# Strassen's seven block products for part of a feed-forward's first multiplication

## The chip, the core and the metric

The kernel runs on one core of a Trainium2 chip. A core has TensorE (matrix products from SBUF into the eight PSUM banks), VectorE, ScalarE and GpSimd (elementwise work), and SyncE, whose queue issues nearly all DMAs of this kernel. The metric is the device time of one execution in microseconds; lower is better. The median of three runs before the change is 756.35 us (755.69 to 757.19).

## The reference, cut to what matters

A layer of a trunk for 512 tokens of width 1024: a token mixer with four groups of heads (mLSTM, short convolution, block attention, HGRN2), a cross-attention to 256 memory rows, and a gated feed-forward, each between two rmsnorms with a residual. The change is in the feed-forward:

```python
def conv_glu_ffn(xn, w_up, conv_w, conv_b, w_down):   # 1024 -> 2 x 2816 -> 1024
    gu = xn @ w_up
    gate, up = jnp.split(gu, 2, axis=-1)
    gate = causal_dwconv(gate, conv_w) + conv_b.astype(gate.dtype)   # 3 taps along the tokens
    return (jax.nn.silu(gate) * up) @ w_down
...
    h = conv_glu_ffn(rmsnorm(x, norm_ffn_pre[l]), ...)
    x = x + rmsnorm(h, norm_ffn_post[l])
```

All data are fp32.

## The kernel before

Products are made in the type fp32r. To keep fp32's accuracy each operand is split into a high part (a rounded copy, written by ScalarE) and a low part (the rest, subtracted by VectorE; `split`, line 483, and `stage`, line 488, for weights), and a product is three matmuls: high x high, high x low, low x high (`three`, line 480).

The normalised tokens lie transposed in `xTh` and `xTl` (partition = channel within one of 8 blocks, columns = 4 token tiles of 128). `norm_T` (line 572) makes them: rms, scaling, a transposition on TensorE into PSUM, and a split. The feed-forward takes the 2816 channels in 22 tiles of 128 (`NF`, loop at line 1138). For a tile f it stages two weight blocks (gate j = 0, up j = 1; 512 KB each), runs 8 x 3 matmuls of 512 columns for each into a PSUM bank, applies the three taps (`act`, two `stt`), Silu and the multiply by `up`, and splits the result into `hT`, which stays in SBUF. Tile 0 alone works on token halves of 256 columns, so that it can begin before the last two token tiles are normalised. The second products (`down`, line 1180) come after all first products (`after=[up_]`): 22 tiles x 4 token tiles x 2 column halves x 3 matmuls of 512 columns, accumulated in all eight banks. The last three tiles are done token tile by token tile, each followed by `residual` (line 1040), which adds to `X[t]` and stores the output.

The order on every engine is worked out by a planner in the program (`Plan`, `schedule`, line 209). Each operation has a cost (`mcost`, line 451, for a matmul; `act`, `dcost` for the others), the planner simulates the engines and the buffers, and always takes the operation that can start earliest; between equals the one with the longest remaining path plus its `boost`. Buffers come from fixed numbers of slots by size: 33 of 4 KB and 10 of 2 KB per partition, and 8 PSUM banks (`SLOTS`, line 38). A unit of operations starts only when the slots that it needs at once are free. A `quota` limits live buffers of a kind (weights 8 tiles ahead for f < 2, then 4; three raw blocks `st`), and a `fifo` keeps the order of loads and of splits. What the planner puts on an engine is executed in that order.

Of the kernel before, what the change touches and what calls it, by code (L numbers as in the profile page):

```python
# [26 lines left out]
P = 128  # L27
# [92 lines left out]
class Plan:  # L120
# [221 lines left out]
def kernel(  # L342
    ctx, tc, x, mem, w_in, b_in, mlstm_norm, rel_bias, hgrn_lb_logits, hgrn_norm,
    w_mix_out, norm_mix_pre, norm_mix_post, mem_norm, w_cq, w_ck, w_cv, w_co,
    norm_cross_pre, norm_cross_post, w_ffn_in, w_ffn_out,
    norm_ffn_pre, norm_ffn_post, c_f, c_m, cols_in, scratch, out,
):
    nc = tc.nc
    pl = Plan()
# [107 lines left out]
    def mms(o, terms, first=True, last=True, spare=0, n=None, quota=(), after=(), boost=0.0, fifo=None, cold=1):  # L457

        def go():
            for j, (l, r) in enumerate(terms):  # L460
                i = nc.tensor.matmul(o.ap(), l.ap(), r.ap(), start=first and j == 0,  # L461
                                     stop=last and j == len(terms) - 1)
# [106 lines left out]
    xTl = sb([P, NT, KT, P], FR, "xTl")  # L569

    @unit
    def norm_T(src, g, dst):
        xs = [sb([P, 512], FT, "xs") for _ in range(2)]
        r = rms([src[:, h * 512:(h + 1) * 512] for h in range(2)], xs)
        for h in range(2):
            hs = slice(h * 512, (h + 1) * 512)
            stt(xs[h].all, src[:, hs], r[:, 0:1], g[:, hs], OP.mult, OP.mult)
        for h in range(2):
            p = ps([P, 4, P])
            for k in range(4):  # L580
# [513 lines left out]
    for t in range(NT):  # L1094
        pl.boost = -5000.0 * t
        qh, ql = qT[t // 2]
        tq = slice((t % 2) * P, (t % 2) * P + P)
        oh_, ol_ = sb([P, 4, P], FR, "oh"), sb([P, 4, P], FR, "ol")
        for hp in range(2):
            with pl.unit():  # L1100
                sp, mx, pr = ps([P, 2, 256]), sb([P, 4], FT, "cmx"), sb([P, 2, 256], FT, "cpr")
                for hh in range(2):
                    h = hp * 2 + hh
                    mms(sp[:, hh, :], three(qh[:, h, tq], ql[:, h, tq], ckh[:, h, :], ckl[:, h, :]), n=256)
                rmax(mx[:, 0:2], sp.all)
# [12 lines left out]
                for hh in range(2):  # L1118
                    h = hp * 2 + hh
                    mms(oT[:, hh, :], [(cv[:, m, h * P:(h + 1) * P], pt[:, hh, m, :]) for m in range(2)])  # L1120
                split(oh_[:, 2 * hp:2 * hp + 2, :], ol_[:, 2 * hp:2 * hp + 2, :], oT.all)
        with pl.unit():
            pp = []
            for c in range(2):
                p, cs = ps([P, 512]), slice(c * 512, c * 512 + 512)
                for k in range(4):
                    wh, wl = wo[k]
                    mms(p.all, three(oh_[:, k, :], ol_[:, k, :], wh[:, 0, cs], wl[:, 0, cs]), k == 0, k == 3,
                        spare=BIG)
                pp.append(p)  # L1130
            xo2 = residual(pp, g_cpost, t)
        norm_T(X[t], g_fpre, into(t))


    pl.boost = 0.0
    g_fpost = gain(norm_ffn_post, [xo2])
    hT = []
    for f in range(NF):
        ww = [stage(wsrc(w_ffn_in, 0, KT, j * DFF + f * P, P), [P, KT, P], 8 if f < 2 else 4) for j in range(2)]
        with pl.unit():  # L1140
            pp = []
            for j in range(2):
                p = ps([P, S])
                wh, wl = ww[j]
                halves = [slice(0, 2), slice(2, 4)] if f < 1 else [slice(0, 4)]
                for hv_ in halves:
                    for k in range(KT):
                        o = p[:, hv_.start * P:hv_.stop * P]
                        up_ = mms(o, three(wh[:, k, :], wl[:, k, :], xTh[:, hv_, k, :], xTl[:, hv_, k, :]),
                                  k == 0, k == KT - 1)  # L1150
                pp.append(p)
            pg, pu = pp
            if f < 4:
                hh, hl = [sb([P, S], FR, "hT") for _ in range(2)]
                vh, vl = hh.all, hl.all
            else:
                hb = sb([P, 2, S], FR, "hT")
                vh, vl = hb[:, 0, :], hb[:, 1, :]
            hT.append((vh, vl))
            w = [cols[:, 22 + 22 * j + f:23 + 22 * j + f] for j in range(3)]  # L1160
            fc = sb([P, S], FT, "fc")
            act(fc.all, pg.all, AF.Copy, scale=w[2])
            stt(fc[:, 1:], pg[:, :S - 1], w[1], fc[:, 1:], OP.mult, OP.add)
            stt(fc[:, 2:], pg[:, :S - 2], w[0], fc[:, 2:], OP.mult, OP.add)
            act(fc.all, fc.all, AF.Silu, bias=cols[:, 88 + f:89 + f])
            tt(fc.all, fc.all, pu.all, OP.mult)
            split(vh, vl, fc.all)

    NL = 3
    wd = []  # L1170
    for f in range(NF):
        src = flat(w_ffn_out, f * P * D, [[D, P], [1, D]])
        if f >= NF - 4:
            i = f - (NF - 4)
            wd.append(stage(src, [P, D], 4, into=(xTh[:, i].re("p k i -> p (k i)"), xTl[:, i].re("p k i -> p (k i)"))))
        else:
            hb, lb2 = stage(src, [P, D], 4)
            wd.append((hb.all, lb2.all))

    def down(o, f, t, c):  # L1180
        ts_, cs = slice(t * P, (t + 1) * P), slice(c * 512, (c + 1) * 512)
# [129 lines left out]
```

## Time and profile before

| what | value |
|---|---|
| median of 3 runs | 756.35 us |
| the profiled execution | 755.57 us, span 753.8 us |
| granted TensorE clock, mean | 0.997 |
| TensorE busy, matmuls | 741.5 us, 4038 |
| VectorE busy | 419.4 us |
| ScalarE busy | 336.8 us |
| DMA | 77.78 MB |
| feed-forward, from tile 0's second half to the last matmul | 385 to 747.5 us |

PE is TensorE's matmuls, PEld its weight loads, DVE VectorE, ACT ScalarE, SP the SyncE queue. The printed duration of a matmul or of a VectorE operation runs from its start to its end; neighbours overlap, so what an instruction takes of its engine is read from the distance between starts. L461 is the line of all products, L478 of transpositions, L386 of all ScalarE operations, L399 of VectorE's two-operand operations, L411 of its operations with a scalar as well (the taps, residuals and scalings).

### The profile page before, as it was taken

What the parts mean: (1) busy time and instruction counts of PE and PEld (TensorE: products, weight loads), DVE (VectorE), ACT (ScalarE), POOL (GpSimd) and SP (SyncE); (2) the same over time, 40 slices, a digit from 0 to 9 for tenths busy, and PEclk for the clock granted to TensorE, in tenths of its full rate; (3) what the DMA queues carried; (4) which work ended last, traced back from release to release, by engine and by line L of the source; (5) the groups of instructions that cost most, each with busy time, mean ns of one, the idle gap of its engine ahead of it and who ended that gap; (6) DMA issues with size and microseconds to landing.
All of it is one profiled execution on the core that took longest, in us unless ns stands there. A gap on an engine that the chain in (4) does not pass through costs nothing.

```text
span 753.8 us, 10351 instructions
## 1 busy us (share of the span) xinstructions
PE 741.5 (98%) x4038; PEld 631.1 (84%) x4038; DVE 419.4 (56%) x799; ACT 336.8 (45%) x662; POOL 35.5 (5%) x65
## 2 busy tenths in 40 slices
PE   7999999999999999999999999999999999999996
PEld 6899989998888988989888888888888888888885
DVE  4879948777664745596755443554344453234005
ACT  5794438437663643485635323344232343123002
POOL 3000210030000000000100000000000000000001
PEclk9999999999999999999999999999999999999998
DMA  8801220500515632243232232223132233245002
GB/s 294 299 1 52 79 92 28 197 29 29 197 57 183 221 126 85 85 140 113 90 107 86 82 93 75 85 85 94 46 111 68 73 88 107 84 167 168 1 0 112
DMA packets 24538, 77.78 MB, mean 103 GB/s; under 512 B 2853, under 2 KB 4517, under 8 KB 24489
## 3 DMA queue, kind: packets, MB, share of 16 engines
q1 hardware_dynamic: 24200, 76.53, 30.7%
q8 instruction: 32, 0.52, 0.3%
q0 software_dynamic: 288, 0.59, 0.3%
q14 instruction: 18, 0.14, 0.1%
HBM read 75.00 MB, written 2.11 MB: 102 GB/s over the span
## 4 chain that ended last, share of the span: by engine, by line
PE 95%; DVE 2%; DMA 1%; SPq 0%; issue 0%; ACT 0%; POOL 0%; DVEq 0%; POOLq 0%; ACTq 0%
PE p L461 91%; PE p L478 3%; DMA st<-in_w_in_dram 1%; PE p L473 1%; DVE at L427 1%; DVE Qt L399 1%; SPq L370 0%; DMA cols<-in_cols_dram 0%; DVE E L399 0%; DVE state L411 0%; DVE xs L411 0%; DVE X L411 0%; DVE xTl L399 0%; POOL rr L564 0%; DVEq L1307 0%
## 5 line engine op out<-in xcount | busy, mean ns | idle before, releaser
L461 PE MATMUL p<-xTh,wh 128*128 128x512 f32 (+1 forms) x560 | 211.8, 378 | 0.2 <-ACT xTh L386 0.2
L461 PE MATMUL p<-xTl,wh 128*128 128x512 f32 (+1 forms) x560 | 210.1, 375 | 0.2 <-DVE xTl L399 0.2
L461 PE MATMUL p<-xTh,wl 128*128 128x512 f32 (+1 forms) x560 | 209.6, 374 | 0.0
L399 DVE TENSOR_TENSOR wl<-st,wh 128x1024 fp32r<-128x1024 f32 (+3 forms) x117 | 138.0, 1194 | 89.2 <-ACT wh L386 74.9
L386 ACT ACTIVATE wh<-st 128x1024 fp32r<-128x1024 f32 (+3 forms) x117 | 117.5, 1031 | 57.7 <-DMA st<-in_w_ffn_out_dram 48.4
L461 PEld LDWEIGHTS p<-xTh,wh 128*128 128x128 f32 x560 | 105.4, 188 | 20.2 <-ACT xTh L386 0.5
L461 PEld LDWEIGHTS p<-xTh,wl 128*128 128x128 f32 x560 | 105.2, 188 | 20.5
L461 PEld LDWEIGHTS p<-xTl,wh 128*128 128x128 f32 x560 | 105.2, 188 | 19.8 <-DVE xTl L399 0.5
L461 PE MATMUL p<-wh,hT 128*128 128x512 f32 x288 | 90.1, 393 | 0.0
L411 DVE SCALAR_TENSOR_TENSOR fc<-p,cols,fc 128x511 f32<-128x511 f32 (+1 forms) x44 | 32.8, 748 | 92.7 <-ACT fc L386 92.0
L461 PEld LDWEIGHTS p<-wh,hT 128*128 128x128 f32 x288 | 54.1, 188 | 12.6
L386 ACT ACTIVATE fc<-p,cols 128x512 f32<-128x512 f32 x22 | 15.0, 684 | 97.9 <-PE p L461 97.9
L461 PE MATMUL p<-wh,xTh 128*128 128x256 f32 (+1 forms) x192 | 56.7, 296 | 0.2 <-ACT xTh L386 0.2
L461 PE MATMUL p<-wl,hT 128*128 128x512 f32 x144 | 56.7, 394 | 0.0
L461 PE MATMUL p<-wh,xTl 128*128 128x256 f32 (+1 forms) x192 | 54.1, 282 | 0.4 <-DVE xTl L399 0.4
L461 PE MATMUL p<-wl,xTh 128*128 128x256 f32 (+1 forms) x192 | 54.0, 281 | 0.0
L399 DVE TENSOR_TENSOR pg<-p,gain 128x512 f32<-128x512 f32 x24 | 16.4, 685 | 52.7 <-ACT sq L386 52.7
L386 ACT ACTIVATE sq<-p 128x512 f32<-128x512 f32 x24 | 14.4, 600 | 67.7 <-PE p L461 67.5
L564 POOL TENSOR_TENSOR rr<-rv,mhalf 128x1 f32<-128x1 f32 x26 | 15.0, 576 | 579.9 <-DVE rv L406 575.4
L461 PEld LDWEIGHTS p<-wh,xTh 128*128 128x128 f32 x192 | 36.3, 189 | 0.9 <-ACT xTh L386 0.5
L461 PEld LDWEIGHTS p<-wh,xTl 128*128 128x128 f32 x192 | 36.2, 188 | 0.6 <-DVE xTl L399 0.6
L461 PEld LDWEIGHTS p<-wl,xTh 128*128 128x128 f32 x192 | 36.2, 189 | 0.5
(236 smaller groups left out, 1085.1 us busy)
## 6 DMA issues: line engine op xcount, KB each, us to landing
st<-in_w_ffn_in_dram SPq DMA_DIRECT2D x44, 512.0 KB, 3.6
st<-in_w_in_dram SPq DMA_DIRECT2D x24, 512.0 KB, 4.7
st<-in_w_ffn_out_dram SPq DMA_DIRECT2D x22, 512.0 KB, 3.6
st<-in_w_mix_out_dram SPq DMA_DIRECT2D x8, 512.0 KB, 3.7
st<-in_w_ck_dram SPq DMA_DIRECT2D x4, 512.0 KB, 5.1
st<-in_w_cv_dram SPq DMA_DIRECT2D x4, 512.0 KB, 5.1
st<-in_w_cq_dram SPq DMA_DIRECT2D x4, 512.0 KB, 4.2
X<-in_x_dram SPq DMA_DIRECT2D x4, 512.0 KB, 5.1
```

Source lines behind the costliest of these rows:

```text
L386: return nc.scalar.activation(o.ap(), i.ap(), func, **kw)
L399: return pl.op(eng, c, lambda: e.tensor_tensor(o.ap(), a.ap(), b.ap(), op=op), reads=[a, b], writes=[o], fifo=fifo, boost=boost)
L411: lambda: nc.vector.scalar_tensor_tensor(o.ap(), a.ap(), ap(s), b.ap(), op0=op0, op1=op1),
L427: return pl.op("DVE", dcost(n, True), lambda: nc.vector.copy_predicated(o.ap(), m.ap(), a.ap()), reads=[m, a, o], writes=[o])
L461: i = nc.tensor.matmul(o.ap(), l.ap(), r.ap(), start=first and j == 0, stop=last and j == len(terms) - 1)
L473: i = nc.tensor.matmul(o[hh * 64:hh * 64 + 64].ap(), l.ap(), r.ap(), start=j == 0, stop=j == len(terms) - 1)
L478: return pl.op("PE", 109.0, lambda: nc.tensor.transpose(o.ap(), a.ap(), idn.ap()), reads=[a, idn], writes=[o])
L564: pl.op("Pool", 470.0, lambda: nc.gpsimd.tensor_tensor(r.all.ap(), v.all.ap(), mhalf[:, :1].ap(), op=OP.pow), reads=[v.all, mhalf.all], wr ...
```

## The change

Tiles 0, 1, 2, 6, 11 and 16 (`PLAIN`) keep 48 matmuls of 512 columns. The other 16 take gate and up as the two row blocks, the two halves of the 1024 input channels as inner blocks, and the two halves of the tokens as column blocks of a 2 x 2 block product, and make it from seven products in place of eight: each is 4 x 3 matmuls of 256 columns (`seven`). The weight sums S1 to S4 are made for every tile, in fp32 on VectorE, and split (`blocks`); the token sums T1 to T4 are made once, when the last two token tiles are normalised, from fp32 copies of the normalised tokens that `norm_T` now keeps (`keep`), and are split into `Th` and `Tl` (8 slots of 4 KB). The products lie in pairs in two banks; ScalarE copies two of the pairs' halves out so that further products can be accumulated on what stays, and VectorE adds the rest into `gu`, from which the taps and the gate go on as before (`glu`).

The gated values are kept in fp32, two tiles to a 4 KB buffer `hP`, and are split only in the second part, at most four tiles ahead, after the second-last tile's last first product. `X[t]` is stored to DRAM (`x2`) after the cross-attention and loaded again after the last first product; the last norm's gain is loaded there too. The planner's matmul cost changes for the whole kernel, and `mms` gets a flag for products that share a bank.

```diff
+PLAIN = (0, 1, 2, 6, 11, 16)
...
         if l.buf.dt == FR:
-            return max(n, 2 * m) / 2.4 + 2.4
+            return max(n, 2 * m) * 0.4445 + 3.7
...
+            if keep:
+                act(keep[h], p.all, AF.Copy)
             split(*dst(h), p.all)
...
+        if t < 2:
+            xf.append([sb([P, 4, P], FT, "xf") for h in range(2)])
+            norm_T(X[t], g_fpre, into(t), [b.all for b in xf[t]])
+        else:
+            with pl.unit():
+                b1, b2 = [sb([P, 4, P], FT, "xf") for h in range(2)]
+                norm_T(X[t], g_fpre, into(t), [b1.all, b2.all])
+                a1, a2 = xf[t - 2]
+                i = t - 2
+                pl.boost -= 60000.0
+                tt(a1.all, b1.all, a1.all, OP.subtract)
+                tt(b1.all, b2.all, b1.all, OP.subtract)
+                tt(b2.all, b2.all, a1.all, OP.subtract)
+                tt(a2.all, a2.all, b2.all, OP.subtract)
+                for j, v in enumerate((a1, b2, b1, a2)):
+                    split(Th[j][:, i], Tl[j][:, i], v.all)
+                pl.boost += 60000.0
+        kept.append(store(flat(x2, t * P * D, [[D, P], [1, D]]), X[t].all, P * D * 4))
...
+    def blocks(g, u):
...
+        high(gh.all, g.all)
+        tt(s1.all, u[:, d1], u[:, d2], OP.add, **k)
+        tt(u[:, d1], g[:, d1], u[:, d1], OP.subtract, **k)
+        high(uh.all, u[:, d2])
+        high(sh[0][:, 0], s1.all)
+        high(sh[0][:, 1], u[:, d1])
+        tt(s2.all, s1.all, g[:, d1], OP.subtract, **k)
+        tt(s4.all, g[:, d2], s2.all, OP.subtract, **k)
+        low(gl.all, g.all, gh.all)
+        high(sh[1][:, 0], s2.all)
+        high(sh[1][:, 1], s4.all)
+        low(sl[0][:, 0], s1.all, sh[0][:, 0])
+        low(sl[0][:, 1], u[:, d1], sh[0][:, 1])
+        low(ul.all, u[:, d2], uh.all)
+        low(sl[1][:, 0], s2.all, sh[1][:, 0])
+        low(sl[1][:, 1], s4.all, sh[1][:, 1])
...
+    def seven(f):
+        W = blocks(*raw(f))
+        with pl.unit():
+            a, b = ps([P, 2, 256]), ps([P, 2, 256])
...
+            prod(b[:, 0], "S1", tblock(0), True)
+            prod(b[:, 1], "S3", tblock(2), False)
+            prod(a[:, 0], "G1", xblock(0, 0), True)
+            prod(a[:, 1], "S2", tblock(1), False)
+            c57 = sb([P, 2, 256], FT, "c57")
+            act(c57.all, b.all, AF.Copy)
+            prod(b[:, 0], "S4", xblock(1, 1), False)
+            o = prod(b[:, 1], "U2", tblock(3), False)
+            c1 = sb([P, 256], FT, "c1")
+            act(c1.all, a[:, 0], AF.Copy)
+            prod(a[:, 0], "G2", xblock(1, 0), False)
+            gu = sb([P, 2 * S], FT, "gu")
+            tt(c1.all, c1.all, a[:, 1], OP.add)
+            act(gu[:, 0:256], a[:, 0], AF.Copy)
+            tt(gu[:, 256:768].re("p (a b) -> p a b", a=2), c1[:, None, :].bc([P, 2, 256]), b.all, OP.add)
+            tt(c57[:, 0], c57[:, 0], c57[:, 1], OP.add)
+            tt(gu[:, 768:], c1.all, c57[:, 0], OP.add)
+            glu(f, gu, gu[:, S:])
...
+            act(hh.all, hP[f // 2][:, f % 2, :], AF.Copy, quota=[("hh", 4)], after=[ups[-2]])
+            tt(hl.all, hP[f // 2][:, f % 2, :], hh.all.cast(FT), OP.subtract)
...
+        X[t] = sb([P, D], FT, "X2")
+        load(X[t].all, flat(x2, t * P * D, [[D, P], [1, D]]), P * D * 4, after=[kept[t], up_])
```

## Rows read from the trace of the kernel before

**Rows 1.** The page's first part: busy us, share, instructions.
```profile
PE 741.5 (98%) x4038; PEld 631.1 (84%) x4038; DVE 419.4 (56%) x799; ACT 336.8 (45%) x662; POOL 35.5 (5%) x65
```

**Rows 2.** Chain that ended last, its last long links: start, us, link.
```profile
385.61 361.92 PE p L461 x1583
747.55 0.60 ACT sq L386
```

**Rows 3.** Windows: A:B, length, busy by engine, clock, DMA share, GB/s.
```profile
357.00:367.00 10.00, 10.00 (x69) 8.96 (x69) 9.05 (x20) 7.04 (x22) 1.10 (x2) 1.00 0.28 105
...
396.00:640.00 244.00, 244.00 (x1065) 198.01 (x1064) 112.25 (x132) 86.05 (x111) 0.00 (x0) 1.00 0.27 84
640.00:747.50 107.50, 107.50 (x465) 86.81 (x463) 28.78 (x32) 21.75 (x30) 1.65 (x3) 1.00 0.26 87
...
700.00:720.00 20.00, 20.00 (x88) 16.27 (x87) 0.00 (x0) 0.00 (x0) 0.00 (x0) 1.00 0.00 1
```

**Rows 4.** Timeline, TensorE: start, us, instruction (first and last of each series).
```profile
378.06 0.28 PE L461 MATMUL p<-xTl,wh 128*128 128x256 f32 x1
...
383.49 0.28 PE L461 MATMUL p<-xTh,wl 128*128 128x256 f32 x1
...
429.80 0.40 PE L461 MATMUL p<-xTh,wl 128*128 128x512 f32 x1
...
447.48 0.39 PE L461 MATMUL p<-xTh,wh 128*128 128x512 f32 x1
```

**Rows 5.** Timeline, VectorE: start, us of all xcount, idle before.
```profile
351.37 0.41 DVE L399 TENSOR_TENSOR ql<-p,qh 128x256 fp32r<-128x256 f32 x1
351.70 0.16 DVE L405 TENSOR_SCALAR cmx<-cmx 128x2 f32<-128x2 f32 x1
...
559.80 1.53 DVE L411 SCALAR_TENSOR_TENSOR fc<-p,cols,fc 128x511 f32<-128x511 f32 x2 [8.66 <-ACT fc L386]
561.25 1.21 DVE L399 TENSOR_TENSOR wl<-st,wh 128x1024 fp32r<-128x1024 f32 x1
...
589.02 2.36 DVE L399 TENSOR_TENSOR wl<-st,wh 128x1024 fp32r<-128x1024 f32 x2 [1.80 <-ACT wh L386]
591.30 1.28 DVE L399 TENSOR_TENSOR fc<-fc,p 128x512 f32<-128x512 f32 x2
```

**Rows 6.** Groups by shape: xcount, busy us, mean ns, idle before, releasers.
```profile
L399 DVE TENSOR_TENSOR wl<-st,wh 128x1024 fp32r<-128x1024 f32 x110 | 132.8, 1221 | 86.7 <-ACT wh L386 72.5 <-PE p L461 14.0
L386 ACT ACTIVATE wh<-st 128x1024 fp32r<-128x1024 f32 x110 | 112.9, 1052 | 53.6 <-DMA st<-in_w_ffn_out_dram 48.4 <-DMA st<-in_w_ffn_in_dram 1.9 <-DMA st<-in_w_in_dram 1.5
...
L461 PEld LDWEIGHTS p<-wh,xTh 128*128 128x128 f32 x192 | 36.3, 189 | 0.9 <-ACT xTh L386 0.5
...
L411 DVE SCALAR_TENSOR_TENSOR fc<-p,cols,fc 128x511 f32<-128x511 f32 x22 | 16.5, 749 | 92.0 <-ACT fc L386 92.0
...
L386 ACT ACTIVATE fc<-fc,cols 128x512 f32<-128x512 f32 x22 | 15.8, 722 | 22.1 <-DVE fc L411 22.1
...
L399 DVE TENSOR_TENSOR hT<-fc,hT 128x512 fp32r<-128x512 f32 x22 | 14.9, 689 | 1.5 <-ACT hT L386 0.7
...
L386 ACT ACTIVATE hT<-fc 128x512 fp32r<-128x512 f32 x22 | 13.7, 631 | 26.8 <-DVE fc L399 26.8
...
L399 DVE TENSOR_TENSOR ql<-p,qh 128x256 fp32r<-128x256 f32 x8 | 3.4, 420 | 7.7 <-ACT qh L386 7.7
```

**Rows 7.** Timeline, TensorE, where the last token tile enters the feed-forward.
```profile
384.89 0.49 PE L461 MATMUL p<-xTh,wh 128*128 128x512 f32 x1 [0.25 <-ACT xTh L386]
385.61 0.50 PE L461 MATMUL p<-xTl,wh 128*128 128x512 f32 x1 [0.23 <-DVE xTl L399]
```

**Rows 8.** DMA issues: KB each, median us from issue to landing.
```profile
X<-in_x_dram SPq DMA_DIRECT2D x4, 512.0 KB, 5.1
```

**Rows 9.** TensorE's waits, first and last of five: us in total, times, longest.
```profile
PE p L478 <- DVE xs L411: 3.5, 4, 1.6
...
PE p L461 <- DVE E L399: 0.2, 1, 0.2
```

More of the change, by code (lines that the diff above doesn't have):

```diff
@@ L345 @@
     norm_cross_pre, norm_cross_post, w_ffn_in, w_ffn_out,
-    norm_ffn_pre, norm_ffn_post, c_f, c_m, cols_in, scratch, out,
+    norm_ffn_pre, norm_ffn_post, c_f, c_m, cols_in, scratch, x2, out,
 ):
@@ L453, in mcost, with mms @@
         if l.buf.dt == FR:
-            return max(n, 2 * m) / 2.4 + 2.4
+            return max(n, 2 * m) * 0.4445 + 3.7
         return max(n, m) / 0.6 + 4.8
-    def mms(o, terms, first=True, last=True, spare=0, n=None, quota=(), after=(), boost=0.0, fifo=None, cold=1):
+    def mms(o, terms, first=True, last=True, spare=0, n=None, quota=(), after=(), boost=0.0, fifo=None, cold=1, open_=False):
         def go():
@@ L461, in go @@
                 i = nc.tensor.matmul(o.ap(), l.ap(), r.ap(), start=first and j == 0,
-                                     stop=last and j == len(terms) - 1)
+                                     stop=last and j == len(terms) - 1, skip_group_check=open_)
             return i
@@ L1078 @@
     CS = 128.0 ** -0.5
+    kept, xf, Th, Tl = [], [], *([sb([P, 2, 4, P], FR, n) for j in range(4)] for n in ("Th", "Tl"))
     qT = []
@@ L1131, with glu, plain @@
             xo2 = residual(pp, g_cpost, t)
-        norm_T(X[t], g_fpre, into(t))
-    pl.boost = 0.0
-    g_fpost = gain(norm_ffn_post, [xo2])
-    hT = []
-    for f in range(NF):
+        if t < 2:
[16 more added lines that the diff above has]
+        kept.append(store(flat(x2, t * P * D, [[D, P], [1, D]]), X[t].all, P * D * 4))
+    pl.boost = 0.0
+    hP = []
+    def glu(f, gate, up):
+        if f % 2 == 0:
+            hP.append(sb([P, 2, S], FT, "hT"))
+        w = [cols[:, 22 + 22 * j + f:23 + 22 * j + f] for j in range(3)]
+        fc = sb([P, S], FT, "fc")
+        act(fc.all, gate[:, :S], AF.Copy, scale=w[2])
+        stt(fc[:, 1:], gate[:, :S - 1], w[1], fc[:, 1:], OP.mult, OP.add)
+        stt(fc[:, 2:], gate[:, :S - 2], w[0], fc[:, 2:], OP.mult, OP.add)
+        act(fc.all, fc.all, AF.Silu, bias=cols[:, 88 + f:89 + f])
+        tt(hP[f // 2][:, f % 2, :], fc.all, up, OP.mult)
+    def plain(f):
         ww = [stage(wsrc(w_ffn_in, 0, KT, j * DFF + f * P, P), [P, KT, P], 8 if f < 2 else 4) for j in range(2)]
@@ L1151 @@
                 pp.append(p)
[L1152 to L1167, printed above, removed]
+            glu(f, pp[0], pp[1].all)
+        return o
+    def raw(f):
+        with pl.unit():
+            st = [sb([P, KT, P], FT, "st", kind="st") for j in range(2)]
+            for j in range(2):
+                load(st[j].all, wsrc(w_ffn_in, 0, KT, j * DFF + f * P, P), P * D * 4, fifo="st", quota=[("st", 4)])
+        return st
@@ new lines, in blocks, with high, low @@
+    @unit
+    def blocks(g, u):
+        d1, d2 = slice(0, 4), slice(4, 8)
+        k = dict(fifo="wl", boost=5000)
+        s1, s2, s4 = (sb([P, 4, P], FT, "su") for j in range(3))
+        gh, gl = sb([P, KT, P], FR, "wh", kind="w"), sb([P, KT, P], FR, "wl")
+        uh, ul = sb([P, 4, P], FR, "uh", kind="w"), sb([P, 4, P], FR, "ul")
+        sh, sl = ([sb([P, 2, 4, P], FR, n) for j in range(2)] for n in ("sh", "sl"))
+        def high(h, v):
+            act(h, v, AF.Copy, fifo="wh", boost=5000)
+        def low(l, v, h):
+            tt(l, v, h.cast(FT), OP.subtract, **k)
+        high(gh.all, g.all)
[14 more added lines that the diff above has]
+        low(sl[1][:, 1], s4.all, sh[1][:, 1])
+        one_ = lambda b, j: [b[:, 4 * j + i] for i in range(4)]
+        two = lambda b, j: [b[:, j, i] for i in range(4)]
+        return dict(G1=(one_(gh, 0), one_(gl, 0)), G2=(one_(gh, 1), one_(gl, 1)), U2=(one_(uh, 0), one_(ul, 0)),
+                    S1=(two(sh[0], 0), two(sl[0], 0)), S3=(two(sh[0], 1), two(sl[0], 1)),
+                    S2=(two(sh[1], 0), two(sl[1], 0)), S4=(two(sh[1], 1), two(sl[1], 1)))
@@ new lines, in xblock, with tblock, prod @@
+    def xblock(k, t):
+        return [(xTh[:, 2 * t:2 * t + 2, 4 * k + i, :], xTl[:, 2 * t:2 * t + 2, 4 * k + i, :]) for i in range(4)]
+    def tblock(j):
+        return [(Th[j][:, :, i, :], Tl[j][:, :, i, :]) for i in range(4)]
+    def seven(f):
+        W = blocks(*raw(f))
+        with pl.unit():
+            a, b = ps([P, 2, 256]), ps([P, 2, 256])
+            def prod(o, w, xs, first):
+                return mms(o, [q for i in range(4) for q in three(W[w][0][i], W[w][1][i], *xs[i])], first, n=256, open_=True)
+            prod(b[:, 0], "S1", tblock(0), True)
[16 more added lines that the diff above has]
+            glu(f, gu, gu[:, S:])
+        return o
@@ L1169 @@
+    ups = [plain(f) if f in PLAIN else seven(f) for f in range(NF)]
+    up_ = ups[-1]
+    g_fpost = gain(norm_ffn_post, [up_])
     NL = 3
-    wd = []
+    wd, hT = [], []
     for f in range(NF):
@@ L1178 @@
             wd.append((hb.all, lb2.all))
+        with pl.unit():
+            hh, hl = sb([P, S], FR, "hh", kind="hh"), sb([P, S], FR, "hl")
+            act(hh.all, hP[f // 2][:, f % 2, :], AF.Copy, quota=[("hh", 4)], after=[ups[-2]])
+            tt(hl.all, hP[f // 2][:, f % 2, :], hh.all.cast(FT), OP.subtract)
+            hT.append((hh, hl))
     def down(o, f, t, c):
@@ L1186 @@
     od = [[ps([P, 512]) for c in range(2)] for t in range(NT)]
+    for t in range(NT):
+        X[t] = sb([P, D], FT, "X2")
+        load(X[t].all, flat(x2, t * P * D, [[D, P], [1, D]]), P * D * 4, after=[kept[t], up_])
     for f in range(NF - NL):
```

12 lines of the change are left out of this document (6 added, 6 removed).

## The prediction

> **What bounds the kernel now.** Read the busy table first: TensorE is busy for 741.5 of 753.8 us, VectorE for 56% and ScalarE for 45% [rows 1]. A busy TensorE need not be a full one, so the chain of waits comes next: its last long link is one unbroken run of matmuls of 361.92 us from 385.61 us, the whole feed-forward, after which only the last residual remains [rows 2]. The windows say the same: in 396 to 640 us, nearly all of it first products, TensorE is busy for 244.00 of 244.00 us, VectorE for 112.25, ScalarE for 86.05 [rows 3]. So the feed-forward lasts as long as its matmuls take to issue, and a change there is worth what it takes off that count, unless it makes VectorE late.
>
> **The term that the change is for.** The price of a matmul is the distance between starts, not its printed duration. With 512 columns: 76 distances from 429.80 to 447.48 us, 0.2326 each; over the whole run I use 0.232. With 256 columns: 46 distances from 378.06 to 383.49 us, 0.118 each, and each of those loads its own 128x128 block of weights, as many loads as matmuls [rows 1, 4]. A plain channel tile is 2 x 8 x 3 = 48 matmuls of 512: 48 x 0.232 = 11.14 us. A Strassen tile is 7 products x 4 x 3 = 84 matmuls of 256: 84 x 0.118 = 9.91 us. Difference 1.22 us, 16 times: **-19.6 us**. The smaller matmul loses almost nothing (2 x 0.118 is 0.236 against 0.232).
>
> The Trainium skill, TensorE: Matmul & The Clock Gate, section Back-to-back issue gap, gives a sustained spacing in real kernels of about 131 ns at 512 columns and 81 ns at 128, that is, a large part that doesn't shrink with the columns; as an estimate from that page, 256 columns would be near 98 ns and a Strassen tile would cost more (8.2 us) than a plain one (6.3 us). The spacings of [rows 4] disagree at both sizes; what it would mean here, a part of a matmul that doesn't shrink, is the last of the rivals.
>
> **VectorE, the engine that pays.** Its price is again the distance between starts. Two multiplies of 512 print 1.28 us together, the second about 0.68, so 0.60 apart; two 1024-wide subtractions print 2.36, so 1.14 apart; a 256-wide one at 351.37 is followed at 351.70, 0.33; the pair of convolution taps, the second needing the first, starts at 559.80 and the next operation at 561.25, 1.45 [rows 5]. A Strassen tile asks of VectorE:
> - weights: 4 sums of 512 and 5 low parts of 512 (9 x 0.60) and one low part of 1024 (1.14): 6.54 us;
> - putting the products together: one of 512 and three of 256 (0.60 + 3 x 0.33): 1.59;
> - taps 1.45 and the gating multiply 0.60: 2.05.
>
> Sum 10.18 us against TensorE's 9.91: VectorE is 0.27 us short on each. A plain tile asks 2 x 1.14 + 2.05 = 4.33 of 11.14 and leaves 6.8 us. The plain tiles 0, 1, 2, 6, 11, 16 cut the others into runs of 3, 4, 4, 5, so the longest run falls 1.4 us behind, less than a plain tile leaves. Over the whole stage: VectorE 16 x 10.18 + 6 x 4.33 + 9.6 (the four token blocks: two times 4 sums and 4 low parts of 512) = 198 us, TensorE 16 x 9.91 + 6 x 11.14 = 225. If VectorE may work ahead, nothing is lost; if it can't, 16 x 0.27 = 4.3 us. Working ahead needs buffers: a Strassen tile holds six 4 KB slots of 33 beside 8 for the token blocks and up to 11 for gated values, so late in the stage two sets fit and a third doesn't. I take **+2** (0 to 4.3). ScalarE: by its durations [rows 6] one copy of 1024 (1.05), five weight copies of 512 (0.63 each), a copy, the scaling and Silu of 512 (at most 0.72 each), two copies of 256 (under 0.63 each): at most 7.6 us of 9.91, hidden. New waits inside a tile: S4's product into bank b waits for ScalarE's copy of b, G2's into a for the copy of a; behind each stand the tile's other matmuls on TensorE, and 24 matmuls on the other bank (2.83 us) lie between. They cover a copy of 0.6 us and one of 1.05 ahead of it; if ScalarE stands behind a late VectorE, that cover goes, which belongs to the range.
>
> **The way into the stage.** At 384 us TensorE waits 0.25 and 0.23 us for the last token tile, behind a ScalarE copy and a VectorE subtraction [rows 7]. The change adds one ScalarE copy of 512 per half ahead of or behind the split: at most 2 x 0.6 more, and one VectorE op of 0.60 may stand in the way. 0 to 2; I take **+1**. Before that the four kept token halves hold 4 of ten 2 KB slots from the first two tiles on, and the third tile's unit asks for eight free 4 KB slots, while softmax, rms and norm of the last tiles still need theirs. TensorE has wo's 24 matmuls of 0.232 per tile (5.6 us) as cover there. VectorE is already at 9.05 of 10 us in 357 to 367 [rows 3]. If one tile's chain is put off beyond the cover, that is up to one wo block, 5.6 us; 0 to 6, I take **+1**, as the last chain (rms, norm, transposition) ends just when its consumer needs it [rows 7].
>
> **The way out, the rest.** The split of gated values moves behind the second-last tile: ScalarE 0.6 and VectorE 0.60 per tile beside 1.14 for the weights, 1.74 of 24 x 0.232 = 5.57 us; VectorE has 28.78 of 107.50 us there [rows 3]: hidden. The last two tiles' assembly must clear two banks each before the eight second products are all open; the free banks give 3 x 0.232 each, 2.8 to 4.2 us. 0 to 2, I take **+0.5**. Residual: four stores and four loads of 512 KB on SP's queue; a load of that kind lands in 5.1 us [rows 8], and from 700 to 720 us the DMA engines' share is 0.00 [rows 3], so even 20 us of delay would not show; a store waiting for its residual can hold the weight loads queued behind it for as long as one residual chain; I take **0**, and the 0 to 6 above holds it. The final gain's later load likewise 0.
>
> The planner's new TensorE prices reorder the kernel before the feed-forward. TensorE's waits that the trace names, five rows, sum to 6.0 us over the span, from 3.5 down to 0.2 [rows 9]: -1.5 (part of the 3.5 for xs) to +3 (half of the 6.0 again); I take **0**.
>
> **Sum.** -19.6 + 2 + 1 + 1 + 0.5 + 0 = -15.1. The profiled execution took 755.57 us (span 753.8 and 1.8 around it), 0.8 below the median of 756.35: 755.57 - 15.1 = 740.5, on the median's footing 741.3, say 741. All the terms' ends at once give 735 and 754 (-21.1 and -2.3).
>
> **Rivals.**
> - *Everything hides*: 736. For it: VectorE's 198 of 225 us. Against: the slots.
> - *The last cross-attention tiles starve of slots*: one or two tiles' chains in the open, 6 to 11 us beyond my terms: 747 to 752. For it: VectorE's 9.05 of 10 there; against: eight slots come free once the last softmax is done, before wo's last block.
> - *VectorE takes over* (the other side). If its ops came at their printed durations, 9 x 0.69 + 1.22 + 0.69 + 3 x 0.42 + 2 x 0.75 + 0.69 = 11.57 us a tile, and the slots allowed no work ahead, each Strassen tile would cost 0.43 more than a plain one: 16 x 0.43 + 2.5 (the ways in and out) = +9.4, 766. It decides from 10.98 us a tile on (11.14 less 2.5/16). For it: the sums are chains, each needing the one before, and ScalarE's in-order queue couples the two engines. Against: the spacings of [rows 5], and a stretch at 90% [rows 3]. The Trainium skill, VectorE: DVE Perf Modes, section The DRAIN you can't avoid, says that the next operation doesn't start until the pipe is empty; by that rule the printed durations would count. The pairs in [rows 5] don't agree with it.
> - *Weight loads bind at 256 columns*, so that a matmul takes the 189 ns of a load [rows 6]: 84 x 0.189 = 15.9, 16 x 4.7 = +76, about 832. The 46 distances of [rows 4] all but exclude it.
>
> **How the numbers follow.** Forecast 0.63 (own range 736 to 747), everything hides 0.11, slots 0.13, VectorE 0.11, weight loads 0.02. Left out of 735 to 753 are VectorE's and the weight loads' cases and some 0.04 at the ends, less than 2 in 10. About 0.2% (1.5 us) is what a measurement can tell. Faster: 0.63 + 0.11 + 0.10 = 0.84; same: 0.01 of the slots' case and 0.03 of VectorE's = 0.04; slower 0.12.
>
> **What would show it.** Right: 84 starts 0.118 apart per Strassen tile, two tiles in 21.1 us; VectorE over 90% busy in the runs and TensorE without idle time; feed-forward from its first product to the last in some 345 us. Wrong: TensorE idle with VectorE's low parts or assembly as releaser inside runs (VectorE's rival); idle time before tile 0 behind norm or slots; 256-column starts wider than 0.12.

## The result, and the profile after

The changed kernel takes 748.27 us (median of 4 runs, 747.11 to 748.70); the kernel before, run beside it, 756.02 (755.11 to 757.19). The ratio is 0.9894, 95% interval 0.9876 to 0.9912: faster by 1.1%, where 741.0 in a range of 735 to 753 was forecast. The profiled executions: span 753.8 before, 745.3 after, so 8.5 us of the forecast 15.1 (7.8 by the medians).

The page's first part, after. TensorE has 576 matmuls more (16 tiles x 36) in 14 us less, and VectorE went from 419.4 to 522.6 us [rows 1]:

```profile
PE 727.7 (98%) x4614; PEld 647.4 (87%) x4614; DVE 522.6 (70%) x1007; ACT 389.1 (52%) x790; POOL 35.5 (5%) x65
```

TensorE's timeline after, late in the first products, is the counterpart of [rows 4]. From 568.52 to 570.38 lie eight distances of 0.2325, from 600.26 to 602.27 seventeen of 0.118. So both prices of the sum held. The last row is a stall, 1.77 us from start to start. And the 512-wide products, which are plain tile 16's, stand among the 256-wide ones of the Strassen tiles behind it: the planner uses a plain tile's products as filler. The last nine of them run from 591.83 to 593.91; the 168 matmuls behind them, tiles 20 and 21, have none between them.

```profile
568.41 0.27 PE L462 MATMUL p<-Th,ul 128*128 128x256 f32 x1
568.52 0.39 PE L462 MATMUL p<-xTh,wh 128*128 128x512 f32 x1
...
570.38 0.40 PE L462 MATMUL p<-xTh,wl 128*128 128x512 f32 x1
570.61 0.28 PE L462 MATMUL p<-Th,sh 128*128 128x256 f32 x1
...
600.26 0.28 PE L462 MATMUL p<-Th,uh 128*128 128x256 f32 x1
...
602.27 0.28 PE L462 MATMUL p<-Th,sl 128*128 128x256 f32 x1
604.04 0.39 PE L462 MATMUL p<-xTh,wh 128*128 128x256 f32 x1 [1.49 <-ACT c L387]
```

The windows after, columns as in [rows 3]. The first row is the way into the stage: TensorE idle for 2.1 us, VectorE at 96%, the granted clock at 0.84. In 400 to 600 us TensorE has no idle time and VectorE is at 86%, in 545 to 600 at 89%. From 594 on, the tiles without filler, VectorE is at 94% and TensorE idle for 2.0 us. The last row are the second products:

```profile
385.00:396.00 11.00, 8.86 (x51) 7.24 (x50) 10.52 (x19) 6.08 (x14) 1.53 (x1) 0.84 0.90 326
400.00:600.00 200.00, 200.00 (x1482) 190.24 (x1481) 172.51 (x274) 107.56 (x181) 0.00 (x0) 1.00 0.27 90
545.00:600.00 55.00, 55.00 (x422) 52.87 (x421) 49.08 (x78) 29.61 (x51) 0.00 (x0) 1.00 0.26 84
594.00:616.30 22.30, 20.33 (x168) 19.87 (x167) 20.90 (x34) 12.88 (x21) 0.00 (x0) 1.00 0.48 161
620.00:738.00 118.00, 118.00 (x511) 95.47 (x510) 45.24 (x56) 34.55 (x52) 1.65 (x3) 1.00 0.25 82
```

The difference of the two traces by TensorE's starts. Half 1 of tile 0 is the last series of 256-column matmuls that doesn't need the last token tile; "entry" is from its last start to the start of the first `xTl` product of the last token tile:

| stretch | before | after | difference |
|---|---|---|---|
| start to the end of half 1 | 383.49 | 388.18 | +4.7 |
| entry | 383.49 to 385.61 | 388.18 to 392.36 | +2.1 |
| entry to the first second product | 239.45 | 224.07 | -15.4 |
| second products, first to last | 122.07 | 122.22 | +0.2 |

In the third line lie 1.3 us of slow clock right after the entry (seven distances of 512-wide matmuls, 3.05 us in place of 1.73: 0.34 and six of 0.232) and two stalls, 1.77 and 0.75 us from start to start, 2.3 us beyond a matmul's spacing. Without them it is -19.0, against the -19.6 that the arithmetic gave.

The entry, after: all engines in the timeline of 388 to 395 us.

```profile
386.63 0.69 DVE L400 TENSOR_TENSOR xf<-xf,xf 128x512 f32<-128x512 f32 x1
...
386.80 1.53 POOL L565 TENSOR_TENSOR rr<-rv,mhalf 128x1 f32<-128x1 f32 x1 [3.30 <-DVE rv L407]
...
387.23 0.69 DVE L400 TENSOR_TENSOR Tl<-xf,Th 128x512 fp32r<-128x512 f32 x1
...
388.36 1.41 DVE L412 SCALAR_TENSOR_TENSOR xs<-X,rr,gain 128x512 f32<-128x512 f32 x2 [0.44 <-POOL rr L565]
...
389.26 1.29 PE L479 MATMUL p<-ident,xs 128*128 128x128 f32 x8 [0.79 <-DVE xs L412]
389.69 2.01 DVE L400 TENSOR_TENSOR xf<-xf,xf 128x512 f32<-128x512 f32 x3
...
389.98 0.60 ACT L387 ACTIVATE xf<-p 128x512 f32<-128x512 f32 x1 [3.67 <-PE p L479]
390.48 0.59 ACT L387 ACTIVATE xTh<-p 128x512 fp32r<-128x512 f32 x1
...
391.12 0.50 PE L462 MATMUL p<-xTh,wh 128*128 128x512 f32 x1 [0.57 <-ACT xTh L387]
...
391.62 1.28 DVE L400 TENSOR_TENSOR xTl<-p,xTh 128x512 fp32r<-128x512 f32 x2
...
392.36 0.79 PE L462 MATMUL p<-xTl,wh 128*128 128x512 f32 x1 [0.74 <-DVE xTl L400]
...
393.38 0.63 PE L462 MATMUL p<-xTh,wh 128*128 128x512 f32 x1
...
393.81 0.63 PE L462 MATMUL p<-xTl,wh 128*128 128x512 f32 x1
```

Three delays stand in it. GpSimd's power for the last token's rms (`rr`) takes 1.53 us and ends only after two operations that VectorE runs beside it, a token sum (`xf`) and the low part of another (`Tl`); in the kernel before it takes 0.55, and the transpositions start 0.11 us after half 1 where they now start 1.08 after. ScalarE's copy `xf` stands ahead of the split `xTh` (389.98, then 390.48). And VectorE's three sums from 389.69 stand ahead of `xTl` (391.62). Behind them matmuls of 512 columns come 0.43 apart where 0.232 is usual: the lower of the clock's two levels, 1.2 GHz, beside 2.4, which makes the mean of 0.84 in the window of 385 to 396. The same GpSimd operation, timeline of the kernel before:

```profile
381.86 0.55 POOL L564 TENSOR_TENSOR rr<-rv,mhalf 128x1 f32<-128x1 f32 x1 [2.97 <-DVE rv L406]
```

TensorE's waits for ScalarE's copies of product halves (`c`), after: us in total, times, longest.

```profile
PE p L462 <- ACT c L387: 2.0, 2, 1.5
```

ScalarE's timeline at the longer of the two waits for `c`, and the start of the weight sums of the last tile on VectorE. The 256-wide copy that frees the bank for tile 20's G2 stands behind six others, four for the weights of the last tile (21) and two of gated values (`hh`) for the second part:

```profile
600.08 1.04 ACT L387 ACTIVATE wh<-st 128x1024 fp32r<-128x1024 f32 x1
601.03 0.62 ACT L387 ACTIVATE uh<-st 128x512 fp32r<-128x512 f32 x1
601.55 0.62 ACT L387 ACTIVATE hh<-hT 128x512 fp32r<-128x512 f32 x1
602.07 0.61 ACT L387 ACTIVATE sh<-su 128x512 fp32r<-128x512 f32 x1
602.59 0.61 ACT L387 ACTIVATE sh<-st 128x512 fp32r<-128x512 f32 x1
603.11 0.61 ACT L387 ACTIVATE hh<-hT 128x512 fp32r<-128x512 f32 x1
603.63 0.36 ACT L387 ACTIVATE c<-p 128x256 f32<-128x256 f32 x1
```

```profile
600.82 0.68 DVE L400 TENSOR_TENSOR su<-st 128x512 f32<-128x512 f32 x1
```

The order on TensorE leaves this copy no cover. In tiles 20 and 21 the seven products run S1, S3, G1, S4, U2, S2, G2: S2, which writes the same bank as G2, stands directly ahead of it. In tile 19 the twelve matmuls of S4, on the other bank, lie between (587.63 to 588.92), and the prediction counted on 24. At tile 21 ScalarE was idle when S2 ended, and the stall is 0.75 us from start to start; at tile 20 the copy starts 1.0 us later behind S2 than there. Two `hh` copies, 0.52 us each, stand ahead of it; what they wait for in the plan, `ups[-2]`, is tile 20's U2 and not its last product. ScalarE's copy at tile 21, and TensorE's G2 behind it:

```profile
614.46 0.38 ACT L387 ACTIVATE c<-p 128x256 f32<-128x256 f32 x1 [0.78 <-PE p L462]
```

```profile
614.90 0.39 PE L462 MATMUL p<-xTh,wh 128*128 128x256 f32 x1 [0.47 <-ACT c L387]
```

### The profile page after: what moved, and what is told of

Read it like the earlier page. It is cut to its first block, busy times and chain, and to the rows that moved or that the text cites. A ratio compares the mean times of both kernels' runs of the same rounds, so it can differ in the third digit from the quotient of the medians.

```text
span 745.3 us, 11908 instructions
## 1 busy us (share of the span) xinstructions
PE 727.7 (98%) x4614; PEld 647.4 (87%) x4614; DVE 522.6 (70%) x1007; ACT 389.1 (52%) x790; POOL 35.5 (5%) x65
## 4 chain that ended last, share of the span: by engine, by line
PE 85%; DVE 7%; ACT 5%; issue 2%; DMA 1%; POOL 0%; SPq 0%; DVEq 0%; POOLq 0%; ACTq 0%
PE p L462 81%; PE p L479 3%; DMA st<-in_w_in_dram 1%; PE p L474 1%; ACT wh L387 1%; DVE at L428 1%; DVE wl L400 1%; DVE Qt L400 0%; ACT e L387 0%; POOL rr L565 0%; DVE xTl L400 0%; DVE X L412 0%; DVE pg L400 0%; DVE E L400 0%; DVE sl L400 0%
## 5 line engine op out<-in xcount | busy, mean ns | idle before, releaser
L462 PE MATMUL p<-xTh,wh 128*128 128x512 f32 (+1 forms) x432 | 147.4, 341 | 2.5 <-ACT c L387 2.0
L462 PE MATMUL p<-xTl,wh 128*128 128x512 f32 (+1 forms) x432 | 145.7, 337 | 0.7 <-DVE xTl L400 0.7
L462 PE MATMUL p<-xTh,wl 128*128 128x512 f32 (+1 forms) x432 | 145.3, 336 | 0.0
L462 PEld LDWEIGHTS p<-xTh,wh 128*128 128x128 f32 x432 | 81.7, 189 | 10.8 <-ACT c L387 2.4
L462 PE MATMUL p<-wh,hh 128*128 128x512 f32 x144 | 56.7, 394 | 0.0
L462 PE MATMUL p<-wh,hl 128*128 128x512 f32 x144 | 56.7, 394 | 0.0
L462 PE MATMUL p<-wl,hh 128*128 128x512 f32 x144 | 56.7, 394 | 0.0
L462 PE MATMUL p<-Th,sl 128*128 128x256 f32 x192 | 54.0, 281 | 0.0
L462 PE MATMUL p<-Th,sh 128*128 128x256 f32 x192 | 53.9, 281 | 0.0
L462 PE MATMUL p<-Tl,sh 128*128 128x256 f32 x192 | 53.9, 281 | 0.0
L400 DVE TENSOR_TENSOR hl<-hT,hh 128x512 fp32r<-128x512 f32 x22 | 15.1, 690 | 52.8 <-ACT hh L387 52.8
```

The costliest lines, as they stand in the source:

```text
L400: return pl.op(eng, c, lambda: e.tensor_tensor(o.ap(), a.ap(), b.ap(), op=op), reads=[a, b], writes=[o], fifo=fifo, boost=boost)
```

## The experiments

Each was timed in three rounds (4 runs) beside the kernel before (7 runs in each group of runs: medians 756.63, 756.39, 755.48).

**The planner's price.** The changed kernel with the earlier matmul price.

```diff
-            return max(n, 2 * m) * 0.4445 + 3.7
+            return max(n, 2 * m) / 2.4 + 2.4
```

> The changed kernel with the planner's old matmul prices, all else as changed. In the changed kernel TensorE starts tile 0's first half at 382.7 us, before the change at 378.1, so 4.7 us are lost ahead of the feed-forward. Theory A (the new prices reorder the stages before): tile 0 starts near 378 again and the time is about 743.5 us, perhaps with up to 3 us given back inside the Strassen tiles, whose plan then rests on prices 7% too low. Rival B (kept token copies and their slots hold up the cross-attention): start and time stay at 382.7 and 748.

744.01 us (743.37 to 746.71), ratio 0.9847 [0.9825, 0.9868]. Half 1 ends at 385.25 in place of 388.18, although in this execution the clock fell for a short stretch some 12 us after the start. The entry is unchanged at 4.2 us and `rr` at 1.53; the first of the late stalls is 2.12 us and there are three.

**The price alone.** The kernel before with the new price (the same two lines the other way round), nothing else.

> The kernel before, with the new matmul prices as its only edit. Theory A (prices): tile 0's first half moves from 378.1 to about 382.7 us and the time from 756.0 to about 760.5. Rival B (copies and slots): both stay, 756.

761.53 us (760.94 to 762.78), ratio 1.0076 [1.0058, 1.0095]: the price by itself costs 4.9 us. TensorE's timeline of that kernel at the end of half 1 and the entry: 388.20 where the changed kernel has 388.18, and an entry of 2.1 us as before the change.

```profile
388.20 0.29 PE L461 MATMUL p<-xTh,wl 128*128 128x256 f32 x1
...
390.34 0.50 PE L461 MATMUL p<-xTl,wh 128*128 128x512 f32 x1 [0.22 <-DVE xTl L399]
```

So the price alone makes the whole loss ahead of the feed-forward. The token halves kept in slots cost 0.5 us there at most: in the version of 740.3 us below, which has them and the earlier price, half 1 ends at 383.94, in the kernel before at 383.49. TensorE starts 2446 matmuls up to that point in all three kernels, not in one order. By the windows it is busy for 378.1 us of them before, 381.1 after and 381.3 here, and idle for 5.5, 7.2 and 7.0: only a third of the loss is idle time, the rest is the same matmuls standing wider apart in another order. It comes in pieces: of the 4.7 us here, 1.6 lie between the 200th and the 500th start, 1.5 between the 1100th and the 1400th, 1.0 between the 2000th and the 2200th.

**The copy behind the split, in program order.**

```diff
+            split(*dst(h), p.all)
             if keep:
                 act(keep[h], p.all, AF.Copy)
-            split(*dst(h), p.all)
```

> The changed kernel with the fp32 copy of the normalised tokens behind the split, not ahead of it, in program order. From the end of tile 0's first half to the flow of its second half the changed kernel takes 4.2 us where it took 2.1 before, and then 8 matmuls at half the granted clock (0.43 for 0.232 us). Theory: the copies ahead of the two splits on ScalarE make 1.0 of it and the clock's fall follows from the longer pause; time 748.3 - 1.0 - 1.5 = about 746. Rival: the pause is made by the chain of the last residual and norm, which VectorE's token sums hold up, and 748 stays.

747.22 us (746.47 to 749.05), ratio 0.9886 [0.9868, 0.9904]. The planner put every engine's instructions into the order that the changed kernel has: the edit moved nothing and tests nothing. It is a second timing of the same program, and shows one thing: here the slow clock lay some 12 us after the start and none at the entry, although the pause there was as long (4.2 us); half 1 ended at 389.55 (1.4 later) and the span was again 745.4. The window of that execution, to compare with the first row of the windows after:

```profile
385.00:396.00 11.00, 8.87 (x61) 7.58 (x61) 10.52 (x19) 7.32 (x16) 1.53 (x1) 1.00 0.78 278
```

**No Strassen tile.** `PLAIN` holds all 22; token sums, kept copies, gated values and price stay.

```diff
-PLAIN = (0, 1, 2, 6, 11, 16)
+PLAIN = tuple(range(22))
```

> The changed kernel with all 22 tiles plain: no Strassen products and no weight sums; the token copies, token sums, fp32 gated values, parked residual and new prices stay. Theory: the Strassen tiles are worth 16 x 1.22 = 19.6 us less 2.2 us of stalls at tiles 20 and 21, so 748.3 + 17.4 = 765.7, which is slower than before the change by what the rest costs (some 9 us). Rival: part of the 19.6 is lost inside the Strassen tiles on VectorE, and this kernel takes 758 or less.

763.36 us (762.57 to 764.00), ratio 1.0095 [1.008, 1.011]. So the sevens are worth 15.1 us net (16.1 against the second timing), where 17.4 was expected: of the 19.6, 2.3 go in the late stalls and 0.5 in an entry that is 3.7 us here and 4.2 with them. The other 0.7 to 1.7 us isn't pinned down; the profiled executions have a short fall of the clock each, at different places. What stays of the change costs 6.7 against the kernel before, 4.9 of it the price.

**Nineteen Strassen tiles.**

```diff
-PLAIN = (0, 1, 2, 6, 11, 16)
+PLAIN = (0, 1, 2)
```

> The changed kernel with plain tiles 0, 1, 2 alone: 19 Strassen tiles in one run, with no plain tile to catch up in. TensorE's count falls by 3 x 1.22 = 3.7 us more. Theory (VectorE, 10.18 us a tile against TensorE's 9.91, is what limits a long run): VectorE falls 19 x 0.27 = 5.1 us behind, its buffers give out, and TensorE waits for ScalarE's and VectorE's copies in the run; the time is 748 to 751, no better than with 16. Rival (all hides as long as the sums are near each other): 747.7 - 3.7 = 744.

750.35 us (749.13 to 751.42), ratio 0.9918 [0.9900, 0.9937]: three tiles more, which by TensorE should give 3.7, cost 2.1. TensorE's waits and a window of that kernel: plain products end at 451 us, and behind them VectorE is full (54.09 of 55 us, after the change 49.08) and TensorE loses 2.5 us in that window; the waits for `sl` and `c` sum to 5.9, after the change to 2.0. The 3.0 for `sl`, VectorE's low parts, lie inside the run, from 521 us on; the 2.9 for `c` are the last two tiles'. The rest of the loss is in part the clock's: its profiled execution has a second short fall, at 607 us.

```profile
PE p L462 <- DVE sl L400: 3.0, 4, 1.1
PE p L462 <- ACT c L387: 2.9, 2, 2.5
```

```profile
545.00:600.00 55.00, 52.52 (x441) 51.90 (x440) 54.09 (x93) 30.70 (x55) 0.00 (x0) 1.00 0.26 82
```

**The token sums later.** Earlier price; the sums and their splits stand behind the loop over the token tiles and wait for the last split.

```diff
-            with pl.unit():
-                b1, b2 = [sb([P, 4, P], FT, "xf") for h in range(2)]
...
+            xf.append([sb([P, 4, P], FT, "xf") for h in range(2)])
+            done = norm_T(X[t], g_fpre, into(t), [b.all for b in xf[t]])
...
+    for i in range(2):
+        with pl.unit():
+            (a1, a2), (b1, b2) = xf[i], xf[i + 2]
+            tt(a1.all, b1.all, a1.all, OP.subtract, after=[done])
...
```

> The kernel with the old prices (744.0 us), with the token sums of the last two token tiles taken out of the loop: they wait for the last tile's split. In the changed kernel and in the one with old prices GpSimd's power for the last token tile takes 1.53 us, before the change 0.55, and VectorE's token sums of two SBUF operands run beside it; then the entry into tile 0's second half takes 4.2 us where it took 2.1. Theory (the sums hold GpSimd up): the power is back at 0.55, the entry at 3.2, and the time near 743. Rival (GpSimd's duration is an accident of its order): it stays at 1.5 and the time at 744. All kept copies live longer in the ten 2 KB slots, which may cost up to 1 us ahead of it.

744.45 us (743.52 to 745.14), ratio 0.9840 [0.9824, 0.9857], as the earlier price alone. GpSimd's `rr` is back at 0.55 and the transpositions start 0.33 us after half 1, but the expected entry of 3.2 us was missed, it is still 4.0: the matmuls wait 1.78 us for `xTh`, since ScalarE's copies still stand ahead of both splits. GpSimd and TensorE at the entry, that kernel's timeline:

```profile
382.93 0.55 POOL L565 TENSOR_TENSOR rr<-rv,mhalf 128x1 f32<-128x1 f32 x1 [2.85 <-DVE rv L407]
```

```profile
385.07 1.06 PE L479 MATMUL p<-ident,xs 128*128 128x128 f32 x8
387.92 0.50 PE L462 MATMUL p<-xTh,wh 128*128 128x512 f32 x1 [1.78 <-ACT xTh L387]
```

**The copies bound behind the splits, alone.** Earlier price, sums where the change has them.

```diff
-            if keep:
-                act(keep[h], p.all, AF.Copy)
-            split(*dst(h), p.all)
+            o = split(*dst(h), p.all)
+            if keep:
+                act(keep[h], p.all, AF.Copy, after=[o])
```

> The earlier prices, the token sums where the change has them, but ScalarE's kept copies bound behind each split's low part. Two things keep TensorE at the entry: GpSimd's pow beside VectorE's token sums (1.53 us in place of 0.55) and ScalarE's copies ahead of the splits. Theory: the copies are the one that ends last, the pow is a second price of 1.0 us beside it: pow still about 1.5, the entry 3.1 (2.1 as before the change and 1.0), no copy ahead of a split, 741 to 743. Rival: the copies are all of the entry and the pow's delay lies beside something else: entry 2.1, 740 to 741. Second rival: the sums on VectorE are enough by themselves: entry 4.0 or more, 744.

744.25 us (744.1 to 745.3), ratio 0.9847 [0.9830, 0.9863]. The entry is 2.96 us, as expected, but by another way: `rr` is at 0.55, because the sum now waits for the later copy and starts as GpSimd finishes. The 0.8 us that remain over 2.1 are VectorE's sums ahead of the scaling `xs` and ahead of `xTl`, in that kernel's VectorE timeline:

```profile
384.22 0.69 DVE L400 TENSOR_TENSOR xf<-xf,xf 128x512 f32<-128x512 f32 x1 [0.54 <-ACT xf L387]
384.83 1.41 DVE L412 SCALAR_TENSOR_TENSOR xs<-X,rr,gain 128x512 f32<-128x512 f32 x2
386.16 0.68 DVE L400 TENSOR_TENSOR Tl<-xf,Th 128x512 fp32r<-128x512 f32 x1
386.76 0.68 DVE L400 TENSOR_TENSOR xf<-xf,xf 128x512 f32<-128x512 f32 x1
387.36 0.68 DVE L400 TENSOR_TENSOR xTl<-p,xTh 128x512 fp32r<-128x512 f32 x1
```

The time didn't follow, and the forecast of 741 to 743 missed: in the new order two late distances are 1.21 and 2.55 us (the longest with the earlier price alone was 2.12), and the profiled execution has a second short fall of the clock behind them.

**Both, with the earlier price throughout.** The last two edits together.

> Token sums behind the last split and copies bound behind the splits, with the earlier matmul prices through the whole kernel, the feed-forward too (the version of 740.3 us had the new ones there). Theory: the 4 us between 744.45 and 740.3 came from the copies alone: entry 2.1, the clock without a fall there, 740 to 741. Rival: the new prices inside the feed-forward gave part of it: entry 2.1, but 742 to 743, with the stall at the last two channel tiles above 1.96 us or another inside the runs.

743.04 us (742.87 to 743.21), ratio 0.9831 [0.9817, 0.9846]. The entry is 2.13 us, as in the kernel before. Four late distances, 1.20, 2.57, 0.64 and 0.76 us, remain.

**Both, with the new price inside the feed-forward.**

```diff
-            return max(n, 2 * m) / 2.4 + 2.4
+            return max(n, 2 * m) * 0.4445 + 3.7 if pl.ffn else max(n, 2 * m) / 2.4 + 2.4
```

> As the kernel with the sums later, and the fp32 copies now bound behind each split by a dependence, so that they can't stand ahead of it on ScalarE; matmul prices old before the feed-forward and new inside it. Theory (copies ahead of the split make 1.0 us of the entry): entry 2.2 us, as before the change, time 1 us under the kernel with the sums later, about 742. Rival (ScalarE had time for them): no change against it.

740.30 us (739.69 to 740.88), ratio 0.9786 [0.9771, 0.9801]. Entry 2.1 us, no fall of the clock there. Against the kernel above, whose price is the only difference, the stretch from half 1's end to the first second product is 1.6 us shorter (225.9 against 227.5); 0.7 lies ahead of it, where the other's profiled execution had an early fall of the clock. So of the 4.2 us from 744.45 to 740.30 the copies brought 1.4 by the medians, and the price inside the stage 1.6 by the profiled executions. What is left lies with the clock at least in part: TensorE's order up to half 1 is the same in both kernels, and the mean granted clock was 0.998 to 0.999 in the four runs here and 0.995 to 0.996 in the four of the other. Waits of the kernel with the earlier price throughout, and then of this one:

```profile
PE p L462 <- ACT c L387: 2.8, 2, 2.3
PE p L462 <- DVE sl L400: 1.3, 2, 0.9
```

```profile
PE p L463 <- ACT c L388: 2.6, 3, 1.7
```

**The last tile plain.** The kernel above, the plain tiles placed so that the runs are 5, 7 and 4 and the last tile is plain.

```diff
-PLAIN = (0, 1, 2, 6, 11, 16)
+PLAIN = (0, 1, 2, 8, 16, 21)
```

> As the kernel with the copies later, with the plain tiles 0, 1, 2, 8, 16, 21 in place of 0, 1, 2, 6, 11, 16: still 16 Strassen tiles, in runs of 5, 7, 4, and the last tile plain. In the changed kernel TensorE waits 1.5 and 0.6 us at tiles 20 and 21. Theory (late slots: tile 21's weight sums begin only 12.4 us after tile 20's, while both tiles' copies stand on ScalarE): these waits go and the time falls by about 2 us, to 740. Rival (VectorE's deficit of 0.27 us a tile makes them): the run of seven shows such waits instead and the time stays.

738.22 us (738.15 to 738.76), ratio 0.9758 [0.9742, 0.9775]: the fastest of all, 18 us below the kernel before. The late stalls are gone, and the run of seven has none: between tile 20's S2 and its G2 now lie 36 products of plain tile 21, from 595.37 to 603.76. They cover the missing matmuls and ScalarE's queue alike, so this run doesn't tell the two apart. Its busy times, its waits for `c` and its TensorE timeline there:

```profile
PE 725.4 (98%) x4614; PEld 647.7 (88%) x4614; DVE 521.4 (71%) x1007; ACT 390.2 (53%) x790; POOL 35.4 (5%) x65
```

```profile
PE p L463 <- ACT c L388: 0.4, 1, 0.4
```

```profile
595.25 0.28 PE L463 MATMUL p<-Th,sl 128*128 128x256 f32 x1
595.37 0.40 PE L463 MATMUL p<-xTh,wh 128*128 128x512 f32 x1
...
603.76 0.28 PE L463 MATMUL p<-xTh,wh 128*128 128x256 f32 x1
```

## Why the prediction was right, and where it was not

The time lies inside the stated 735 to 753, but outside the forecast's own 736 to 747. That it is inside is in part luck: the room at the top was kept for slots and for VectorE, which needed little of it, and a term put at 0 took 4.9 us.

- **The main term, -19.6: right.** Both spacings held, 256 columns at 0.118 and 512 at 0.232, with no idle TensorE in 400 to 600 us. Without the slow clock and the stalls the stretch lost 19.0; leaving the sevens out costs 15.1 net. The rival in which weight loads bind (832) is refuted by 17 distances of 0.118.
- **The planner's price, 0 (bounds -1.5 to +3): the step that failed.** It measured +4.9 by itself. The bounds came from TensorE's idle time, 6.0 us of named waits. The loss is mostly not idle time: 3.0 to 3.2 us are the same matmuls standing wider, and no list of waits bounds that. It is spread over many groups of operands, none of which grew by over 0.9 us (the 40 transpositions of `pr` the most); why the new order puts them wider stays open. The new price is the truer one: it gives 231.3 and 117.5 ns for the two shapes against 232 and 118 measured, the earlier one 215.7 and 109.1.
- **The way in, +1 (0 to 2): mis-sized.** The entry grew by 2.1 us, and in the profiled execution 1.3 us of slow clock followed. One ScalarE copy of 0.5 ahead of `xTh` and VectorE's sums ahead of `xTl` (0.5) are in the prediction. GpSimd's power, 0.98 longer, is not: the step looked at the queues of two engines and not at what runs beside the third. The experiments show all three: sums moved alone leave 4.0 us, copies bound alone 2.96, both 2.13.
- **Slots in the last cross-attention tiles, +1 (0 to 6): nearly nothing.** Half 1 ends at 388.20 without any kept token halves and at 388.18 with them; with the earlier price it is 383.49 and 383.94. The measured 748 lies in that rival's 747 to 752 for other reasons; its mechanism is refuted.
- **VectorE's deficit, +2 (0 to 4.3): the size near (2.3), the mechanism another, so the agreement is luck.** The prediction saw runs of Strassen tiles that a plain tile lets catch up afterwards. In the trace the plain products stand inside the runs as filler, and while there are any, nothing is lost. Both stalls, at tiles 20 and 21 behind the last filler, are waits for ScalarE's copy and not for VectorE. The cover that failed is the 24 matmuls between: the planner put S2 there, in the same bank, and of the 2.3 us some 1.3 are the copy's bare delay (0.63 at each tile) and 1.0 ScalarE's queue, with tile 21's weights and two `hh` ahead of tile 20's copy. That S2 comes last fits the planner's rule (the whole second part hangs on U2, which gives U2 the longest remaining path); no run tests it. With tile 21 plain the stalls are gone; with three tiles fewer plain they grow. There the deficit itself shows too: 0.27 x 19 = 5.1 us was the arithmetic, and TensorE waited 3.0 us for `sl`. Why tile 21's sums start as late as 600.82, 12.5 us after tile 20's (slots, or the load's quota), was not isolated.
- **VectorE takes over (766): wrong for these runs, right as a limit.** Sixteen keep it at 86%, under the 90% that the prediction named as a sign; nineteen with no filler put it at 98% of a window and lose time. In the VectorE timeline of the copies' experiment 512-wide operations print 0.68 and start 0.60 apart. The Trainium skill, VectorE: DVE Perf Modes, section The DRAIN you can't avoid, has the next operation wait until the pipe is empty, by which printed durations would count, and adds that an operation that is not held starts earlier; these rows agree with the addition alone.
- **The way out, +0.5; residual in DRAM, 0: right.** The second products take 122.2 us against 122.1, and TensorE is busy for 118.0 of 118.0 us there.

From the last token tile's entry to the last matmul the stage takes 346.3 us against 361.5: -15.2. The terms for this stretch (-19.6, +2, +0.5) make -17.1; the 1.9 between them are 1.3 of slow clock and 0.6 of the main term. The rest of the error is what the change does ahead of it: 4.7 by the price and 2.1 at the entry, where +2 was put for both the entry and the slots. One of the prediction's signs is summed wrongly: 21.1 us is a Strassen tile and a plain one, two Strassen tiles are 19.8.

## What to carry to other kernels

The term that was instructions times the distance between their starts held. A planner's cost model is not free to change, even to truer values: here the same price cost 4.9 us in one part of the kernel and gained 1.6 in another, and a run with that line alone shows it where idle time doesn't. Where a new stage begins, list everything that the change puts on each in-order engine in the last few microseconds before it, the small GpSimd operation on the chain too, and bind what isn't urgent behind what is. Where a product must wait for a copy out of its own bank, look in the planned order, and not in the program's, for what stands between. Work that asks little of the second engine is worth keeping for the very end of the stage: as filler it hid that engine's deficit and the copies here, and the tiles behind the last of it stood in the open.

## What the runs showed of the hardware

GpSimd's power of a 128x1 column takes 0.55 us alone and 1.53 beside two of VectorE's operations that read both operands from SBUF; in the five versions timed with sums or copies moved it is 0.55 again, and with no Strassen tile, where one such operation runs beside it, it is 0.93. The kernel before has such rows too, 0.99 at 18.85 us. The Trainium skill, SBUF — State Buffer, section Who interferes with whom, says that a VectorE instruction with two SBUF inputs contends with a GpSimd instruction that reads SBUF; the trace agrees, by up to 0.98 us here.

TensorE's granted clock fell to its lower level for a short stretch in most profiled executions, at different places: behind the entry's pause in three versions (the changed kernel, nineteen tiles, sums later), 11 to 17 us after the start in six (one of them the second execution of the changed kernel's program), and a second time behind the late stalls of 2.55 and 2.74 us in two (the copies alone, nineteen tiles), while a stall of 2.57 us in the version with both edits and the earlier price had no fall behind it. By the starts of the same matmuls with and without it, or by their usual spacing, a fall cost between 0.8 and 1.7 us. Neither the execution profiled of the kernel before nor those of the price alone and of the 740.3 us version have one inside; how much of it belongs to the change is open.
